# Sixteen small loads, a limit on products between weight tiles, and a norm that uses TensorE

## The chip, the cores and the metric

The kernel runs on one core of one Trainium2 chip. The metric is the device time of one execution in microseconds. TensorE (PE) multiplies, VectorE (DVE), ScalarE (ACT) and GpSimd (POOL) do the element work, and SyncE (SP) issues most of the DMA transfers between device memory and the on-chip memories.

## The reference, cut to what matters

One inference step of a one-layer decoder trunk, in float32. 1032 tokens (1024 new ones of a prompt and 8 single samples) with 2048 features each:

```
mod = silu(c) @ w_ada + b_ada;  shift, scale, gate = split(mod, 3)
h = rmsnorm(x, norm_g) * (1 + scale) + shift
z = h @ w_in                       # 2048 x 8208; the last 16 columns are the logits
...                                # short convolutions, gated delta rule over 8 heads
y = concat(y_a, o) @ w_out;  x = x + gate * y;  return rmsnorm(x, final_norm_g), states
```

`rmsnorm` divides each token by the root of the mean of its squared features. `w_ada` is 2048 x 6144; its first 4096 columns give shift and scale, which h needs, and which depend on no token.

## The kernel before, in words

Features lie on the 128 partitions, in 16 blocks k of 128, and tokens along the free dimension. The tokens are worked in two halves, the first of 512. A product of full precision is three passes on PE: each operand is split in a high part (`whi`, `hh`) and a remainder (`wlo`, `hl`), and high by high, high by remainder and remainder by high are added in PSUM; `passes` is such a triple. ACT makes the high part of a weight tile (`raw` to `whi`), POOL or DVE the remainder (`split_w`). Up to four `raw` tiles are loaded ahead (`Stream.ahead`).

The order of all instructions is written by a planner at build time (`_Order`): it keeps a model of each engine's free time, of the DMA lanes and of each tile's readiness, and side generators (`spawn`) are stepped when their time has come in that model. `_transfer` gives a transfer's modelled time: 290 GB/s for long pieces, 210 for pieces of 512 bytes, 66 for some columns of `w_in`. Each engine executes its own list in order; SP too issues its loads in order, and a load waits for its buffer and for the completion counter that it is to use, of which there are eight for all DMAs.

The ramp is the part around the change. First the 16 blocks of the first half of x are loaded, and `norm` squares them on ACT and adds the squares on DVE into `acc`. `rstd_of` then sums `acc` over the partitions on PE, takes the power -1/2 on POOL, writes the result on the diagonals of `dg` (DVE), and spreads it over all partitions by a product with ones (PE); ACT copies it to `rstd`.

Meanwhile 64 tiles of `w_ada`, `wat`, 512 KB each, stream in with up to nine in flight (`load_ada`). The ramp has ten steps of one or two feature blocks, (0), (1), (2, 3), ... (12, 13), (14), (15). For a step PE multiplies the conditioning by four or eight tiles into `ps`, ACT copies it to `ev`, PE sums four row groups (`selada`), DVE adds the biases (`sh`, `s1`), and `make_h` makes hh and hl of the step's blocks: x times rstd (DVE), scale and shift (ACT and DVE), remainder (DVE). Each h block brings seven triples, of seven output columns that are accumulated in seven PSUM tiles through the whole ramp (`first_products`). `fill` puts such triples into PE's list ahead of a `wat` product, for as long as the planner expects the tile not to have landed.

The logits' 16 columns of `w_in` (`lr`, 2048 rows of 64 bytes) are loaded in the ramp's third step by one DMA that ACT issues; they are used at the ramp's end, as `wlt`.

Of the kernel before, what the change touches and what calls it, by code (L numbers as in the profile page):

```python
# [8 lines left out]
F32 = mybir.dt.float32  # L9
F32R = mybir.dt.float32r  # L10
AF = mybir.ActivationFunctionType
ALU = mybir.AluOpType
# [79 lines left out]
class _Order:  # L92
# [11 lines left out]
    def __init__(self):  # L104
        self.free = dict.fromkeys(("P", "V", "S", "G", "Y", "SH", "YH"), 0.0)
        self.seen, self.slots, self.side, self.busy = {}, {}, [], []
        self.step_end = 0.0
        self.port = {"V": [], "G": []}
        self.lanes, self.lane = [0.0] * 8, 0
        self.pinned = set()  # L110

    @property
    def now(self):
# [198 lines left out]
class _Engine:  # L312
# [15 lines left out]
    def enter(self, op, args, kw, aps, r):  # L328
        od = self.od
        out = [aps[0]] + ([kw["accum_out"]] if kw.get("accum_out") is not None else [])  # L330
        ins = aps[1:] if len(out) == 1 else [a for a in aps[1:] if a is not out[1]]
        n = max(_size(a) for a in aps)
        psum = any("PSUM" in str(a.space) for a in aps)
        one = len([a for a in ins[1:] if _size(a) == 1 and n > 1])
        if op == "dma_start":
            od.move(self.key, ins[0], out[0], _transfer(ins[0], out[0]))
            return
        if self.key == "V":
            if op in ("tensor_scalar", "tensor_copy", "memset"):
# [44 lines left out]
def _trunk(ctx, tc, nc, xT, w_in, w_ada, w_out, pack, consts, vecs, csq, ssm, yT, cap, cqp, ssp, cas, cqs, sss):  # L384
# [76 lines left out]
    def rstd_of(acc, n, out, now=False):  # L461

        nf, w = n // P, n % P
        sm = tp.tile([P, 8], F32, tag="rs", name="rsm")
        if w:
            G.memset(sm[:], 1.0)
        yield [acc[:, :n], 2 * MARGIN]
        while held["ch"]:
            yield 0.2
        ps = ch_tile()  # L470
        for c in range(nf):
            mm(ps[:, c:c + 1], acc[:, c * P:(c + 1) * P], ones[:, 0:1], start=True, stop=True)
        if w:
            mm(ps[:w, nf:nf + 1], acc[:, nf * P:n], ones[:, 0:1], start=True, stop=True)
            V.tensor_scalar(sm[:w, nf:nf + 1], ps[:w, nf:nf + 1], 1.0 / D, EPS, ALU.mult, ALU.add)
        V.tensor_scalar(sm[:, :nf], ps[:, :nf], 1.0 / D, EPS, ALU.mult, ALU.add)
        yield
        nc_ = nf + (1 if w else 0)
        G.tensor_tensor(sm[:, :nc_], sm[:, :nc_], nhalf[:, :nc_], ALU.pow)
        yield  # L480
        dg = tp.tile([P, WH], F32, tag="fx", name="dg", bufs=FX)
        V.tensor_tensor(dg[:, :nf * P].rearrange("p (c i) -> p c i", i=P), ident.unsqueeze(1).to_broadcast([P, nf, P]),
                        sm[:, 0:nf].unsqueeze(2).to_broadcast([P, nf, P]), ALU.mult)
        if w:
            V.tensor_scalar(dg[:w, nf * P:n], ident[:w, :w], sm[:w, nf:nf + 1], None, ALU.mult)
        yield
        p2 = ch_tile()
        mm(p2[:, :nf * P], ones[:], dg[:, :nf * P], start=True, stop=True)
        if w:
            p3 = p2[:, nf * P:n] if n <= 512 else ch_tile()[:, :w]  # L490
            mm(p3, ones[:w, :], dg[:w, nf * P:n], start=True, stop=True)
        S.activation(out[:, :nf * P], p2[:, :nf * P], AF.Copy)
        if w:
            S.activation(out[:, nf * P:n], p3, AF.Copy)
        if now:
            return p2
        yield
# [37 lines left out]
    b1 = cp.tile([P, NK], F32, name="b1")  # L535
    V.tensor_scalar(b1[:], pkv("bada", 16, 16), 1.0, None, ALU.add)

    def make_h(k, xt, n, hh, hl):

        t = tp.tile([P, WH], F32, tag="tm", name="ht")  # L540
        V.tensor_tensor(t[:, :n], xt[:, :n], rstd[:, :n], ALU.mult)
        S.activation(hh[:, :HT], t[:, :HT], AF.Identity, bias=sh[:, k, 0:1], scale=s1[:, k, 0:1])
        V.tensor_scalar(t[:, :HT], t[:, :HT], s1[:, k, 0:1], sh[:, k, 0:1], ALU.mult, ALU.add)
        if n > HT:
            V.tensor_tensor(t[:, HT:n], t[:, HT:n], s1[:, k, 1:9], ALU.mult)
            V.tensor_tensor(t[:, HT:n], t[:, HT:n], sh[:, k, 1:9], ALU.add)
            V.tensor_copy(hh[:, HT:n], t[:, HT:n])
        V.tensor_tensor(hl[:, :n], t[:, :n], hh[:, :n].bitcast(F32), ALU.subtract)
# [13 lines left out]
    class Stream:  # L562
# [26 lines left out]
                self.ahead()  # L589
                yield 0.3  # L590

        def ahead(self, split=True):

            while True:
                if self.loaded < min(self.split + RAW, len(self.todo)):
# [2 lines left out]
                        SY.dma_start(raw[:, a:b, :], src)  # L598
                    self.raws.append(raw)
                    self.loaded += 1  # L600
                elif split and self.split < min(self.freed + SPL, self.loaded) and (
                        self.eager or self.split < self.used + 2 or self.landed()):
                    whi = wp.tile([P, 4, P], F32R, tag="whi", name="whi", bufs=SPL)
                    wlo = wp.tile([P, 4, P], F32R, tag="wlo", name="wlo", bufs=SPL)
# [1 line left out]
                    self.raws[self.split] = None  # L606
                    self.done.append((whi, wlo))
                    self.split += 1
                else:
                    return  # L610

# [769 lines left out]
    def fx_tile(name):  # L1381
        return tp.tile([P, WH], F32, tag="fx", name=name, bufs=FX)

    def norm():
        for k in range(NK):
            if k == 0:
                S.activation(acc[:, :HT], xs0[k][:, :HT], AF.Square)
            else:
                sqt = fx_tile("sqt")
                S.activation(sqt[:, :HT], xs0[k][:, :HT], AF.Square)  # L1390
                V.tensor_tensor(acc[:, :HT], acc[:, :HT], sqt[:, :HT], ALU.add)
        yield from rstd_of(acc, HT, rstd)
        normed.append(True)
    normed = []

    hs = []
    with ExitStack() as pools:
# [35 lines left out]
                        yield  # L1433
        rw, queue, done = {}, [], 0

        def fill(t):

            while od.now < t and queue and od.ready(hs[queue[0][0]][1], False) <= od.now:
                if next(queue[0][1], True):
                    queue.pop(0)  # L1440

        for _ in range(4):
            load_ada()
        ws.ahead(split=False)
        for _ in range(4, ADA):
            load_ada()
        od.spawn(norm())
# [1 line left out]
        for step, (f, nf) in enumerate(steps):  # L1449
            ps = tp_tile()  # L1450
            while done < len(units) and units[done][0] == f:
                _, _, s_, k0, nk = units[done]
                wt = wats[done]
                fill(max(od.ready(wt[:], False), od.ready(ps[:], True) if k0 == 0 and s_ == 0 else 0.0))
                for k in range(k0, k0 + nk):
                    j = k % 4
                    mm(ps[32 * j:32 * j + 32, s_ * nf * P:(s_ + 1) * nf * P], sc[:, k, :],
# [2 lines left out]
                wats[done] = None  # L1460
                done += 1
                load_ada()
                if done < len(units) and units[done][0] == f:
                    pump()
            ev = tp.tile([P, WH], F32, tag="zr", name="ev")
            S.activation(ev[:, :2 * nf * P], ps[:, :2 * nf * P], AF.Copy)
            pump()
# [7 lines left out]
                V.tensor_scalar(s1[:, k, :], ps[:, o:o + 9], b1[:, k:k + 1], pkv("ng", k, 1), ALU.add, ALU.mult)  # L1475
            od.first(ps_g, "tp", ps)
            if step == 0:
                while not normed:
                    od.advance()
                pss = [mm_tile(), mm_tile(), mm_tile(), tp_tile(), ch_tile(), o_tile(), ch_tile()]  # L1480
            if f % 4 == 0:
                hs += h_quad()
            for k in range(f, f + nf):
                make_h(k, xs0[k], HT, *hs[k])
                xs0[k] = None
            queue.append((f + nf - 1, first_products(step)))
            if step == 2:
                S.dma_start(cs[:, EARLY:], consts[:, EARLY:LATE])
                lr_ = fx_tile("lr")
                lr = lr_[:, :256].rearrange("p (k n) -> p k n", n=16)  # L1490
                S.dma_start(lr, w_in[:, 8192:8208].rearrange("(k p) n -> p k n", p=P))
        for _, g in queue:
            for _ in g:
                pass
        S.activation(wl[:, :, 0:16], lr, AF.Copy)
        V.tensor_tensor(wl[:, :, 16:32], lr, wl[:, :, 0:16].bitcast(F32), ALU.subtract)
        ramp = [[p] for p in pss]
        od.spawn(ws.run())

    resd = dp.tile([NK, P, HT], F32, name="resd", bufs=1)  # L1500
# [81 lines left out]
    for half in range(2):  # L1582
# [3 lines left out]
        with ExitStack() as pools:  # L1586
# [100 lines left out]
            if half == 0:  # L1687
# [12 lines left out]
                def next_h():  # L1700

                    for _ in range(2):
# [6 lines left out]
                        make_h(k, x1s[k], WH, *quad[-1][k % 4])  # L1709
# [135 lines left out]
```

## Time and profile before

| | us |
|---|---|
| median of 3 runs | 2210.68 (2208.65 to 2213.19) |
| the profiled execution | 2215.43 |
| its span | 2213.4 |
| PE busy | 2127.4 |
| DVE busy | 1254.3 |
| ACT busy | 829.3 |
| POOL busy | 823.4 |

The span goes from the first to the last instruction on the chip. Busy times of engines lie beside each other and don't sum to the span. In rows of the trace, `a<-b,c` names the tile written and those read; an arrow in brackets names what ended the idle time before an instruction.

### The profile page before, as it was taken

What the parts mean: (1) busy time and instruction counts of PE and PEld (TensorE: products, weight loads), DVE (VectorE), ACT (ScalarE), POOL (GpSimd) and SP (SyncE); (2) the same over time, 40 slices, a digit from 0 to 9 for tenths busy, and PEclk for the clock granted to TensorE, in tenths of its full rate; (3) what the DMA queues carried; (4) which work ended last, traced back from release to release, by engine and by line L of the source; (5) the groups of instructions that cost most, each with busy time, mean ns of one, the idle gap of its engine ahead of it and who ended that gap; (6) DMA issues with size and microseconds to landing.
All of it is one profiled execution on the core that took longest, in us unless ns stands there. A gap on an engine that the chain in (4) does not pass through costs nothing. (4 is left out here: it accounts for less than half of the span.)

```text
span 2213.4 us, 40425 instructions
## 1 busy us (share of the span) xinstructions
PE 2127.4 (96%) x15033; PEld 1865.4 (84%) x15033; DVE 1254.3 (57%) x3664; ACT 829.3 (37%) x1887; POOL 823.4 (37%) x800
## 2 busy tenths in 40 slices
PE   5889999999999999999999999999999999999997
PEld 3457777777777788877889999999999999999996
DVE  3325658637768466258315648657576576335545
ACT  3223434333444333343324334333343333334553
POOL 1122334333333344432434333344333433344444
PEclk9899999999999999999999999999999999999998
DMA  9892685789554455875444565466574445878776
GB/s 291 246 292 58 129 160 144 135 124 144 116 133 89 95 97 94 73 143 187 151 120 101 117 128 113 111 111 107 97 100 82 95 100 96 87 90 230 212 219 202
DMA packets 507318, 299.65 MB, mean 135 GB/s; under 512 B 37361, under 2 KB 486641, under 8 KB 507121
## 3 DMA queue, kind: packets, MB, share of 16 engines
q1 hardware_dynamic: 482352, 285.17, 61.2%
q10 hardware_dynamic: 24768, 11.90, 2.3%
q8 instruction: 118, 1.93, 0.4%
q14 instruction: 80, 0.65, 0.1%
HBM read 277.06 MB, written 19.94 MB: 134 GB/s over the span
## 5 line engine op out<-in xcount | busy, mean ns | idle before, releaser
L322 POOL TENSOR_TENSOR wlo<-raw,whi 128x512 fp32r<-128x512 f32 x528 | 707.0, 1341 | 1279.5 <-ACT whi L322 1105.2
L371 PE MATMUL mm<-hh,whi 128*128 128x264 f32 (+1 forms) x3008 | 975.0, 324 | 9.4 <-DVE y L322 3.8
L371 PE MATMUL mm<-hl,whi 128*128 128x264 f32 (+1 forms) x3008 | 972.7, 323 | 6.5 <-DVE hl L322 6.4
L371 PE MATMUL mm<-hh,wlo 128*128 128x264 f32 (+1 forms) x3008 | 971.0, 323 | 0.5 <-POOL wlo L322 0.5
L322 ACT ACTIVATE whi<-raw 128x512 fp32r<-128x512 f32 x672 | 418.1, 627 | 622.8 <-PE mm L371 349.7
L371 PEld LDWEIGHTS mm<-hh,whi 128*128 128x128 f32 x3008 | 569.1, 189 | 58.8 <-issue 6.9
L371 PEld LDWEIGHTS mm<-hl,whi 128*128 128x128 f32 x3008 | 569.5, 189 | 48.4 <-DVE hl L322 8.9
L371 PEld LDWEIGHTS mm<-hh,wlo 128*128 128x128 f32 x3008 | 569.1, 189 | 41.7 <-POOL wlo L322 1.4
L371 PE MATMUL mm<-yhi,wlo 128*128 128x512 f32 (+2 forms) x768 | 247.9, 323 | 6.3 <-DVE wlo L322 4.7
L371 PE MATMUL mm<-yhi,whi 128*128 128x512 f32 (+2 forms) x768 | 246.1, 320 | 1.3 <-ACT whi L322 1.3
L371 PE MATMUL mm<-ylo,whi 128*128 128x512 f32 (+2 forms) x768 | 246.0, 320 | 0.0
L322 DVE TENSOR_TENSOR ob<-tb,xb 128x62 f32<-128x62 f32 (+30 forms) x992 | 195.6, 237 | 2.6 <-DMA tb<-ub 2.6
L322 DVE TENSOR_TENSOR xb<-xb,ob 128x62 f32<-128x62 f32 (+30 forms) x992 | 196.2, 238 | 0.0
L322 DVE TENSOR_TENSOR wlo<-raw,whi 128x512 fp32r<-128x512 f32 x144 | 110.1, 769 | 133.8 <-ACT whi L322 133.0
L371 PEld LDWEIGHTS mm<-yhi,wlo 128*128 128x128 f32 x768 | 144.4, 188 | 21.7 <-DVE wlo L322 6.7
L371 PEld LDWEIGHTS mm<-yhi,whi 128*128 128x128 f32 x768 | 144.5, 188 | 12.7 <-ACT whi L322 1.6
L371 PEld LDWEIGHTS mm<-ylo,whi 128*128 128x128 f32 x768 | 144.6, 188 | 12.6 <-issue 1.0
L322 DVE SCALAR_TENSOR_TENSOR kq<-zr,pk,kq 128x512 f32<-128x512 f32 x96 | 99.6, 1037 | 3.4
L322 DVE SCALAR_TENSOR_TENSOR res<-mm,ga,xr 128x512 f32<-128x512 f32 (+2 forms) x48 | 27.3, 568 | 109.1 <-PE mm L371 101.8
L371 PE MATMUL tpt<-wat,sc 128*32 128x256 f32 (+1 forms) x640 | 44.9, 404 | 32.9 <-DMA wat<-in_w_ada 29.4
L322 DVE TENSOR_TENSOR acc<-acc,sqt 128x512 f32<-128x512 f32 (+3 forms) x75 | 56.2, 751 | 24.2 <-ACT sqt L322 22.5
L322 DVE SCALAR_TENSOR_TENSOR rt<-cht,gt_neg,v 128x128 f32<-128x128 f32 x56 | 19.6, 350 | 81.0 <-PE cht L371 81.0
(401 smaller groups left out, 1974.7 us busy)
## 6 DMA issues: line engine op xcount, KB each, us to landing
raw<-in_w_in SPq DMA_DIRECT2D x488, 256.0 KB, 5.1
raw<-in_w_out SPq DMA_DIRECT2D x160, 256.0 KB, 3.1
wat<-in_w_ada SPq DMA_DIRECT2D x64, 512.0 KB, 7.7
gw<-in_w_ada SPq DMA_DIRECT2D x64, 256.0 KB, 6.0
tb<-ub ACTq DMA_DIRECT2D x16, 512.0 KB, 6.7
raw<-in_w_in SPq DMA_DIRECT2D x48, 128.0 KB, 6.0
sl<-in_ssm SPq DMA_DIRECT2D x12, 512.0 KB, 6.4
x1s<-in_xT SPq DMA_DIRECT2D x16, 260.0 KB, 5.3
```

The source lines that it names most:

```text
L322: r = f(*args, **kw)
L371: r = self.pe.matmul(out, lhsT, rhs, **kw)
```

## The change

- The planner gets a factor `rings` on every transfer's modelled time, 0.87 during the ramp and 1.0 after it.
- `rstd_of`, which five norms use, no longer makes `dg`: PE transposes each group of 128 values, read with a step of zero as a 128 x 128 tile, and so gets them on all partitions.
- In `norm` the squares of blocks 2, 5, 8 and 11 are summed by PE (a product with the identity) in PSUM, and DVE adds this sum once.
- The multiplication of x by rstd leaves `make_h` for `scaled`; in the ramp it is issued before the `ev` copy, and in the first step it reads the transposes' PSUM tile, not `rstd`. One weight tile is split when the first norm is done.
- `fill` takes a limit: at most three triples ahead of a `wat` product; ahead of a step's first product, while its `ps` tile isn't free, there is none.
- The logits' columns come in sixteen loads of 128 rows (8 KB), issued by SP, one after every third `wat` load from the seventeenth tile used.

```diff
-            od.move(self.key, ins[0], out[0], _transfer(ins[0], out[0]))
+            od.move(self.key, ins[0], out[0], _transfer(ins[0], out[0]) * od.rings)
...
-        dg = tp.tile([P, WH], F32, tag="fx", name="dg", bufs=FX)
-        V.tensor_tensor(dg[:, :nf * P].rearrange("p (c i) -> p c i", i=P), ident.unsqueeze(1).to_broadcast([P, nf, P]),
-                        sm[:, 0:nf].unsqueeze(2).to_broadcast([P, nf, P]), ALU.mult)
-        if w:
-            V.tensor_scalar(dg[:w, nf * P:n], ident[:w, :w], sm[:w, nf:nf + 1], None, ALU.mult)
-        yield
         p2 = ch_tile()
-        mm(p2[:, :nf * P], ones[:], dg[:, :nf * P], start=True, stop=True)
+        for c in range(nf):
+            mm(p2[:, c * P:(c + 1) * P], sm[:, c:c + 1].to_broadcast([P, P]), ident, is_transpose=True)
...
-    def make_h(k, xt, n, hh, hl):
-
+    def scaled(xt, n, r):
         t = tp.tile([P, WH], F32, tag="tm", name="ht")
-        V.tensor_tensor(t[:, :n], xt[:, :n], rstd[:, :n], ALU.mult)
+        V.tensor_tensor(t[:, :n], xt[:, :n], r[:, :n], ALU.mult)
+        return t
+
+    def make_h(k, t, n, hh, hl):
+
...
+            if k in PSQ:
+                mm(ps[:], ident, sqt[:, :HT], start=(k == PSQ[0]), stop=(k == PSQ[-1]))
+                continue
+            V.tensor_tensor(acc[:, :HT], acc[:, :HT], sqt[:, :HT], ALU.add)
+            if k == NK - 3:
+                V.tensor_tensor(acc[:, :HT], acc[:, :HT], ps[:], ALU.add)
+        normed.append((yield from rstd_of(acc, HT, rstd, True)))
+    PSQ, normed = (2, 5, 8, 11), []
...
-        def fill(t):
-
-            while od.now < t and queue and od.ready(hs[queue[0][0]][1], False) <= od.now:
+        def fill(t, most=1000):
+
+            while most and od.now < t and queue and od.ready(hs[queue[0][0]][1], False) <= od.now:
                 if next(queue[0][1], True):
                     queue.pop(0)
+                most -= 1
...
-                fill(max(od.ready(wt[:], False), od.ready(ps[:], True) if k0 == 0 and s_ == 0 else 0.0))
+                if k0 == 0 and s_ == 0:
+                    fill(od.ready(ps[:], True))
+                fill(od.ready(wt[:], False), 3)
...
                 load_ada()
+                k = done - 16
+                if 0 <= k < 48 and k % 3 == 0:
+                    k //= 3
+                    if k == 0:
+                        lr_ = fx_tile("lr")
+                        lr = lr_[:, :256].rearrange("p (k n) -> p k n", n=16)
+                    SY.dma_start(lr[:, k, :], w_in[k * P:(k + 1) * P, 8192:8208])
                 if done < len(units) and units[done][0] == f:
                     pump()
+            if step == 0:
+                while not normed:
+                    od.advance()
+                ws.ahead(1)
+            ts = []
+            for k in range(f, f + nf):
+                ts.append(scaled(xs0[k], HT, rstd if step else normed[0]))
+                xs0[k] = None
             ev = tp.tile([P, WH], F32, tag="zr", name="ev")
             S.activation(ev[:, :2 * nf * P], ps[:, :2 * nf * P], AF.Copy)
...
             if step == 2:
                 S.dma_start(cs[:, EARLY:], consts[:, EARLY:LATE])
-                lr_ = fx_tile("lr")
-                lr = lr_[:, :256].rearrange("p (k n) -> p k n", n=16)
-                S.dma_start(lr, w_in[:, 8192:8208].rearrange("(k p) n -> p k n", p=P))
```

## Rows read from the trace of the kernel before

**Rows 1.** The page, part 1: busy time, share of the span, instructions.
```profile
PE 2127.4 (96%) x15033; PEld 1865.4 (84%) x15033; DVE 1254.3 (57%) x3664; ACT 829.3 (37%) x1887; POOL 823.4 (37%) x800
```

**Rows 2.** Windows: stretch and length; busy of each engine, PE clock, DMA share, GB/s.
```profile
200.00:400.00 200.00, 199.32 (x1226) 156.94 (x1226) 136.21 (x412) 78.93 (x188) 73.45 (x74) 1.00 0.62 135
...
600.00:800.00 200.00, 193.64 (x993) 156.10 (x992) 141.12 (x454) 83.31 (x211) 74.96 (x75) 0.99 0.48 103
...
0.00:63.96 63.96, 34.85 (x295) 21.50 (x295) 21.38 (x42) 19.11 (x32) 7.48 (x14) 0.87 1.02 299
63.96:194.94 130.98, 114.69 (x760) 73.18 (x757) 37.82 (x70) 30.45 (x48) 28.01 (x25) 0.93 0.76 215
```

**Rows 3.** Timeline of PE at the ramp's end: start, duration, engine, line, operation, tiles.
```profile
194.94 0.40 PE L371 MATMUL mm<-hh,wlt 128*128 128x512 f32 x1
```

**Rows 4.** Windows of 2 us.
```profile
62.00:64.00 2.00, 2.00 (x21) 0.71 (x13) 1.11 (x3) 0.89 (x2) 0.00 (x0) 0.50 1.10 349
...
84.00:86.00 2.00, 2.00 (x13) 1.01 (x12) 0.00 (x0) 0.00 (x0) 0.00 (x0) 0.76 0.09 25
```

**Rows 5.** Waits of SP's queue, 40 to 90: total us, times, longest.
```profile
SPq L322 <- DMA lr<-in_w_in: 14.1, 1, 14.1
```

**Rows 6.** The tile lr: its load (issue ns, first and last start), and its landing.
```profile
L322 ACTq DMA_DIRECT2D lr<-in_w_in x1: 618/618/618, 63.2 to 63.2; - x1
...
DMA to landing us min/median/max: 21.6/21.6/21.6
```

**Rows 7.** Timeline of SP's queue: two issues of w_ada tiles.
```profile
84.90 0.37 SPq L322 DMA_DIRECT2D wat<-in_w_ada  x1
...
156.93 0.37 SPq L322 DMA_DIRECT2D wat<-in_w_ada  x1
```

**Rows 8.** Waits of PE, 63.9 to 194.9: total us, times, longest.
```profile
PE mm L371 <- DVE hl L322: 5.7, 5, 1.9
PE tpt L371 <- DMA wat<-in_w_ada: 4.0, 2, 3.5
PE tpt L371 <- ACT ev L322: 2.3, 1, 2.3
PE mm L371 <- ACT hh L322: 1.9, 2, 1.2
PE tpt L371 <- PE tpt L371: 1.9, 2, 1.0
```

**Rows 9.** Timeline of ACT: the copy ahead of the late ev.
```profile
100.62 0.63 ACT L322 ACTIVATE whi<-raw 128x512 fp32r<-128x512 f32 x1 [1.79 <-DMA raw<-in_w_in]
```

**Rows 10.** Windows of 10 us; the granted clock is third from the end.
```profile
80.00:90.00 10.00, 8.25 (x50) 4.59 (x50) 0.00 (x0) 0.11 (x1) 0.00 (x0) 0.83 0.66 189
...
100.00:110.00 10.00, 7.25 (x52) 4.25 (x52) 4.58 (x10) 3.26 (x5) 2.13 (x2) 0.66 1.09 330
...
150.00:160.00 10.00, 10.00 (x52) 5.89 (x51) 0.00 (x0) 1.47 (x3) 2.58 (x2) 0.84 0.98 271
```

**Rows 11.** DMA queues in 68 to 72: packets, MB, share of 16 engines.
```profile
q1 hardware_dynamic: 188, 0.19, 14.7%
q10 hardware_dynamic: 580, 0.04, 8.2%
```

**Rows 12.** Timeline of DVE: the first norm's adds; one multiplication by rstd.
```profile
7.43 11.84 DVE L322 TENSOR_TENSOR acc<-acc,sqt 128x512 f32<-128x512 f32 x15 [1.09 <-ACT sqt L322]
...
141.58 0.68 DVE L322 TENSOR_TENSOR ht<-x,rstd 128x512 f32<-128x512 f32 x1
```

**Rows 13.** Timeline of the last norm: dg, and its product with ones.
```profile
2201.81 0.42 DVE L322 TENSOR_TENSOR dg<-cs,rsm 128x256 f32<-128x256 f32 x1 [0.81 <-POOL rsm L322]
...
2202.29 1.22 PE L371 MATMUL cht<-dg,ones 128*128 128x256 f32 x2 [1.49 <-DVE dg L322]
```

**Rows 14.** Groups by line, shapes apart: busy us, mean ns of one.
```profile
L371 PE MATMUL tpt<-cs,kq 128*128 128x128 f32 x128 | 19.2, 272 | 0.0
...
L371 PE MATMUL cht<-dg,ones 128*128 128x512 f32 x6 | 4.1, 774 | 0.0
```

More of the change, by code (lines that the diff above doesn't have):

```diff
@@ L110, in __init__ @@
         self.pinned = set()
+        self.rings = 0.87
     @property
@@ L480, in rstd_of @@
         yield
-        dg = tp.tile([P, WH], F32, tag="fx", name="dg", bufs=FX)
-        V.tensor_tensor(dg[:, :nf * P].rearrange("p (c i) -> p c i", i=P), ident.unsqueeze(1).to_broadcast([P, nf, P]),
-                        sm[:, 0:nf].unsqueeze(2).to_broadcast([P, nf, P]), ALU.mult)
-        if w:
-            V.tensor_scalar(dg[:w, nf * P:n], ident[:w, :w], sm[:w, nf:nf + 1], None, ALU.mult)
-        yield
         p2 = ch_tile()
-        mm(p2[:, :nf * P], ones[:], dg[:, :nf * P], start=True, stop=True)
+        for c in range(nf):
+            mm(p2[:, c * P:(c + 1) * P], sm[:, c:c + 1].to_broadcast([P, P]), ident, is_transpose=True)
         if w:
             p3 = p2[:, nf * P:n] if n <= 512 else ch_tile()[:, :w]
-            mm(p3, ones[:w, :], dg[:w, nf * P:n], start=True, stop=True)
+            mm(p3, sm[:w, nf:nf + 1].to_broadcast([w, P]), ident[:w, :w], is_transpose=True)
         S.activation(out[:, :nf * P], p2[:, :nf * P], AF.Copy)
@@ L590, in run, with ahead @@
                 yield 0.3
-        def ahead(self, split=True):
+        def ahead(self, most=SPL):
             while True:
@@ L600, in ahead @@
                     self.loaded += 1
-                elif split and self.split < min(self.freed + SPL, self.loaded) and (
+                elif most and self.split < min(self.freed + SPL, self.loaded) and (
                         self.eager or self.split < self.used + 2 or self.landed()):
@@ L1384, in norm @@
     def norm():
+        ps = ch_tile()
         for k in range(NK):
@@ L1387, in norm @@
                 S.activation(acc[:, :HT], xs0[k][:, :HT], AF.Square)
[L1388 to L1394, printed above, removed]
+                continue
+            sqt = fx_tile("sqt")
+            S.activation(sqt[:, :HT], xs0[k][:, :HT], AF.Square)
+            if k in PSQ:
+                mm(ps[:], ident, sqt[:, :HT], start=(k == PSQ[0]), stop=(k == PSQ[-1]))
+                continue
+            V.tensor_tensor(acc[:, :HT], acc[:, :HT], sqt[:, :HT], ALU.add)
[3 more added lines that the diff above has]
+    PSQ, normed = (2, 5, 8, 11), []
     hs = []
@@ L1434, in _trunk @@
         rw, queue, done = {}, [], 0
-        def fill(t):
-            while od.now < t and queue and od.ready(hs[queue[0][0]][1], False) <= od.now:
+        def fill(t, most=1000):
+            while most and od.now < t and queue and od.ready(hs[queue[0][0]][1], False) <= od.now:
                 if next(queue[0][1], True):
                     queue.pop(0)
+                most -= 1
         for _ in range(4):
             load_ada()
-        ws.ahead(split=False)
+        ws.ahead(0)
         for _ in range(4, ADA):
@@ L1477, in _trunk @@
             if step == 0:
-                while not normed:
-                    od.advance()
                 pss = [mm_tile(), mm_tile(), mm_tile(), tp_tile(), ch_tile(), o_tile(), ch_tile()]
@@ L1482, in _trunk @@
                 hs += h_quad()
-            for k in range(f, f + nf):
-                make_h(k, xs0[k], HT, *hs[k])
-                xs0[k] = None
+            for k, t in zip(range(f, f + nf), ts):
+                make_h(k, t, HT, *hs[k])
             queue.append((f + nf - 1, first_products(step)))
@@ L1497, in _trunk @@
         ramp = [[p] for p in pss]
+        od.rings = 1.0
         od.spawn(ws.run())
@@ L1708, in next_h @@
                             yield 0.2
-                        make_h(k, x1s[k], WH, *quad[-1][k % 4])
+                        make_h(k, scaled(x1s[k], WH, rstd), WH, *quad[-1][k % 4])
                         hs.append(quad[-1][k % 4])
```

## The prediction

> **What bounds the kernel now.** I read the page's busy shares first: TensorE (PE) is busy 96% of the span, so little can be won unless one stretch holds the idle 4% [rows 1]. Then the windows: PE idles 0.7 us in 200 to 400, 6.4 in 600 to 800, but far more at the start [rows 2]. Before 63.96 us it is busy 34.85 of 63.96 us while the DMA share is 1.02: that start is bound by w_ada's transfers, and PE starves. From 63.96 to 194.94 us (the first product with the logits' columns, `mm<-hh,wlt`, by which all first products are done [rows 3]) PE is busy 114.69 of 130.98 us, so it idles 16.3, at a mean clock of 0.93, and the DMA share is only 0.76. The reader is to see that in this second stretch neither engine nor DMA is full: something keeps work from PE. All that the change can win lies there and at the very end of the program.
>
> The cause is in the 2-us windows: 349 GB/s at 62 to 64, 25 at 84 to 86 [rows 4]. At 70 us SP, which issues every weight load in order, stops: its longest wait is 14.1 us for the one load of the logits' columns [rows 5], issued by ScalarE at 63.2 us and landing 21.6 us later [rows 6]; its next load goes out at 84.90 [rows 7]. It waits because completion counters are handed round over the DMAs, and the one that its next load needs belongs to that slow load. The last w_ada tile is issued only at 156.93 us [rows 7].
>
> What it costs PE: in 63.96 to 194.94 PE waits 4.0 us for w_ada tiles (3.5 of them in one piece, at the end of the hole) and 2.3 for an `ev` copy [rows 8]. The `ev` wait belongs to the hole as well: ScalarE copies `ev` right behind a `whi` that waited 1.79 us for its own raw tile, late because SP was stopped [rows 9]. The other waits, hl 5.7, hh 1.9 and PE on PE 1.9, are those of a step's boundary. Each stretch of idling is followed by the lower clock: the granted clock is 0.83 in 80 to 90, 0.66 in 100 to 110, 0.84 in 150 to 160 [rows 10], that is, parts of these run at 1.2 GHz and not 2.4, and lose 1.7, 3.4 and 1.6 us.
>
> **The change, part by part** (against the profiled execution: 2215.43 us, span 2213.4; the median of the runs is 2210.68, 4.75 lower).
>
> 1. *The single load goes.* The hole's waits go (4.0 + 2.3 = 6.3), and the low clock after two of them (1.7 + 3.4 = 5.1): minus 11.4 us. Bounds: minus 4.0, the direct waits alone, and minus 16, if all PE idling of the stretch is the hole's. DMA transfers are late next, but far from the end: the last w_ada issue is 38 us before 194.94, and in the meantime PE works off a backlog.
>
> 2. *Sixteen loads of 8 KB come into SP's queue*, one for every three w_ada tiles. They total 2048 pieces of 64 bytes, as before. No row shows them in this queue. Below: 580 of these packets take 8.2% of 16 engines in 4 us [rows 11], 9 ns each, so 128 of them on 16 engines are 0.07 us a load and 1.1 us in all. Above: the old load's whole 21.6 us [rows 6] over sixteen is 1.35 us each, 21.6 in all, if w_ada stands still behind each one; the same rows show that it nearly did: w_ada's queue moved 188 packets in 4 us beside 580 of the small ones. Between them I take 0.7 us a load on the DMA, the middle, 11 us. But PE pays only where it has run dry of landed tiles, and nine tile buffers stand between; with a third of the loads felt I take plus 4 us. The issue itself (0.37 us as a tile's [rows 7], 5.9 in all) I cost at nothing, since SP is ahead of the landings; behind it in SP's queue stand the next `raw` and w_ada loads, and for these PE waits.
> The rows say that 64-byte pieces, not the number of loads, set the price. The Trainium skill, "DMA: Bandwidth & Descriptors", section Rules for kernel authors, says to coalesce many small transfers into one large one, since under 64 KB one pays mostly overhead; that speaks against cutting 128 KB into sixteen. By it sixteen small loads would each carry a completion of their own, and the median would come out at 2213.8, by the upper end above; the trace agrees only that small pieces are dear, the one large transfer being here the one that stops SP.
>
> 3. *At most three triples between tiles, and the planner's transfers times 0.87.* This reorders PE's stream and adds or removes nothing. Per two-k step 14 triples face 8 tiles, so three a tile never starves the step; before, only the planned landing limited them. A full-rate tile (524 KB at 349 GB/s, [rows 4]) lands in 1.5 us, and the planner had priced it at 290 GB/s; 0.87 brings it to 333, near the row. Bounds: minus 5, plus 5; I take 0.
>
> 4. *x times rstd is made ahead of the ev copy.* It takes the 0.68 us multiply [rows 12] out of the chain from `sh`/`s` to hh and hl, once for the first k of a step and again in front of the second. Seven waits on hl and hh sum to 7.6 us [rows 8]; I take half of it, 3.5, and half of the low clock behind the boundary at 142 to 149 (1.6), 0.8: minus 4.3. Bounds: 0 if the boundary then waits for `ev`, minus 10.
>
> 5. *First norm.* VectorE loses four of 15 adds and gains one from PSUM; its adds, 15 in 11.84 us with their gaps, stand from 7.43 to 19.27 [rows 12], so at most 3 x 0.79 = 2.4 us go, and with them `dg`, the ones-product and the copy of rstd behind them. Four squares on PE lie ahead of its first w_ada product, where it has nothing else. I cost all of it at 0: w_ada's transfers, at a share of 1.02 until 63.96, are the cover. Without this cover it would be worth 4 us (2.4, and the 1.70 of step 6).
>
> 6. *The other norms.* Each transpose replaces a share of `dg` and the ones-product. The last norm stands on the path to the end: from `dg`'s start at 2201.81 to the ones-product's end at 2203.51 it is 1.70 us [rows 13]. Transposes of 128x128 are 272 ns alone and 19.2/128 = 0.15 in a row [rows 14]: two take 0.42, so minus 1.3. Two norms of 512 tokens amid a full PE: 4.1/3 = 1.37 us [rows 14] against 0.6, minus 1.5 together. Bounds of all three: minus 1.5, minus 4.
>
> Sum: -11.4 + 4 + 0 - 4.3 + 0 - 1.3 - 1.5 = -14.5, so 2200.9 for a profiled execution and 2196.2 for the median. After 195 us the rest moves as a block, because PE has no slack there.
>
> **Rivals.**
> *A. The small loads hold the ring (slower).* Every one of the sixteen stops the w_ada behind it for 1.35 us, and the planner, which prices it at about a tenth of that, puts w_ada's products in PE's stream where the tile isn't there, with ready triples behind. For it: 188 packets in 4 us [rows 11]. Against: nine buffers, and the 38 us of backlog. Then +21.6 replaces +4: 2213.8, and two more drops of the clock like that of 100 to 110 add 6.8, about 2221. It decides from 1.2 us a load that reaches PE.
> A rule by which it would come about: the Trainium skill, "DMA: Bandwidth & Descriptors", section Queues, rings and completion order, says that one engine's descriptors are consumed in ring order within a queue, while different queues take turns. The old load had a queue of its own; the new ones stand in w_ada's. Whether taking turns was cheaper no run here shows.
> *B. Only the direct wait goes.* PE is then limited at the boundaries, the `ev` and low clock at 100 come back there, and the multiply moved ahead gains nothing: 4.0 + 1.7 + 1.3 = 7, so 2203.7. For it: the hl waits, five, aren't all in the hole's wake. Against: the `whi` that waited for a raw tile [rows 9].
> *C. The gain is lost later.* The new order after the ramp costs what the ramp won: PE's idle time of 200 us differs by 5.7 us between two stretches [rows 2]; two such differences give back 11.4: 2207.6.
> *D. All idling and low clock of the stretch go* (16.3, and 0.07 x 130.98 = 9.2; with the last norm 26.8): 2183.9.
>
> **How the numbers follow.** Forecast 0.60, A 0.09, B 0.18, C 0.08, D 0.05. 0.2% is 4.4 us, about what can be told from no change: faster means below 2206.3. Faster: 0.60, D's 0.05 and most of B, 0.15, make 0.80; within: C and the rest of B, 0.11; slower: A, 0.09. The range goes from D, 2184, to C, 2208; the forecast's own range is 2187 to 2203.
>
> **What would show it.** Right: no SP wait over 3 us for the logits' load; DMA above 250 GB/s in every 10 us from 46 to 140; the first `mm<-hh,wlt` at 176 to 184 us and not 194.94; hl waits at half of 5.7; between the last rsm and rf about 0.5 us and not 1.75. Step 2 is wrong if PE's waits for w_ada after 64 us exceed 6 us, step 4 if hl and hh waits stay at 7.6. The prediction fails if the first `wlt` product comes after 190 us, or if it comes early and PE's idle time after 200 us grows by as much.

## The result, and the profile after

The changed kernel takes 2178.61 us (median of 4 runs, 2177.39 to 2183.28) against 2209.66 for the kernel before on the same chip (4 runs); the ratio is 0.9868, with a 95% interval of 0.9853 to 0.9882. So the direction was right, but the gain is twice the forecast one: 0.0132 x 2209.66 = 29 us instead of 14.5, and the time lies below the range.

Its profiled execution took 2179.28 us. The page's busy shares of the changed kernel:

```profile
PE 2116.6 (97%) x15045; PEld 1858.7 (85%) x15045; DVE 1243.7 (57%) x3653; ACT 829.3 (38%) x1887; POOL 826.4 (38%) x801
```

PE is busy 10.8 us less than in [rows 1] though it has twelve instructions more: 7.9 us less in the second stretch below, where it had been granted a low clock, 2.6 more in the first, and 5.4 less behind the ramp. The windows show it (changed kernel; length, then busy time and count of PE, PEld, DVE, ACT, POOL, then PE clock, DMA share, GB/s). The split is at 59.82 us, the start of a product `mm<-hh,whi` as 63.96 is in [rows 2], and at 169.30, the ramp's end; the two stretches behind it, the 2-us and the 10-us windows are those of [rows 2, 4, 10].

```profile
0.00:59.82 59.82, 37.43 (x296) 21.01 (x296) 21.67 (x40) 20.42 (x34) 7.90 (x15) 0.83 1.03 303
59.82:169.30 109.48, 106.75 (x769) 68.75 (x766) 38.35 (x67) 28.17 (x45) 28.64 (x26) 1.00 0.92 266
200.00:400.00 200.00, 199.71 (x1275) 156.74 (x1274) 141.19 (x471) 78.01 (x194) 73.39 (x75) 1.00 0.66 138
600.00:800.00 200.00, 196.22 (x1044) 158.66 (x1042) 123.46 (x389) 76.00 (x181) 72.98 (x74) 0.99 0.49 98
62.00:64.00 2.00, 2.00 (x21) 0.80 (x19) 1.27 (x3) 0.00 (x0) 0.00 (x0) 1.00 1.10 352
84.00:86.00 2.00, 2.00 (x15) 1.29 (x15) 0.00 (x0) 0.60 (x1) 1.28 (x1) 1.00 1.11 338
80.00:90.00 10.00, 10.00 (x69) 6.56 (x68) 2.21 (x7) 3.27 (x5) 2.46 (x3) 1.00 1.11 345
100.00:110.00 10.00, 10.00 (x68) 6.08 (x67) 5.04 (x10) 3.16 (x5) 2.55 (x2) 1.00 1.11 338
150.00:160.00 10.00, 10.00 (x104) 8.20 (x103) 4.71 (x9) 2.24 (x4) 1.29 (x1) 1.00 0.37 92
```

The reader is to see three things. The second stretch is 21.5 us shorter (109.48 against 130.98): PE idles 2.7 us in it, not 16.3, and at a full clock it is busy 106.75 us, not 114.69. The hole in the transfers is gone: 338 GB/s at 84 to 86, not 25. And the gain is kept: PE idles 0.3 and 3.8 us in the two stretches after the ramp, less than before.

The ramp ends with the first product by the logits' columns. PE's timeline of the changed kernel has it here:

```profile
169.28 0.40 PE L372 MATMUL mm<-hh,wlt 128*128 128x512 f32 x1
```

That is 25.7 us before [rows 3], where the forecast had 11.7 for the ramp (11.4 - 4 + 4.3). What PE still waits for between 59.8 and 169.3 us (line and tile waited for; us in total, times, longest):

```profile
PE mm L372 <- DVE hl L323: 1.8, 3, 1.0
PE tpt L372 <- PE tpt L372: 1.0, 1, 1.0
```

There is no wait for a w_ada tile, for `ev` or for hh any more [rows 8]. SP's waits from 46 to 160 us (first and fourth line of that list) name the logits' tile nowhere; it stands mostly for a free buffer:

```profile
SPq L323 <- PE tpt L372: 16.2, 19, 3.4
...
SPq L323 <- DMA wat<-in_w_ada: 4.0, 7, 0.9
```

The logits' tile itself (min, median, max of the issues in ns, first and last start; then the landing), where [rows 6] had one landing of 21.6 us:

```profile
L323 SPq DMA_DIRECT2D lr<-in_w_in x16: 495/1168/1863, 59.3 to 156.0; - x16
...
DMA to landing us min/median/max: 3.7/6.2/8.0
```

In SP's timeline the last two w_ada tiles go out at 140.64 us, not at 156.93 [rows 7]:

```profile
140.64 2.57 SPq L323 DMA_DIRECT2D wat<-in_w_ada  x2
```

And the last norm has its two transposes where [rows 13] had `dg` and the product with ones (chain of waits):

```profile
2166.28 0.70 POOL rsm L323
...
2167.03 0.45 PE cht L372 x2
```

One thing must be known about the rows of before: a second profile of that kernel has a span of 2206.0 us, not 2213.4, with the ramp's end at 194.4 us, as in [rows 3]. So some 7 us of the difference between the profiles of [rows 2] and of the changed kernel lie after the ramp and belong to the one execution. I compare ramps by their end (194.4 to 169.3, minus 25.1) and totals by the ratio of runs.

### The profile page after: what moved, and what is told of

It reads as the page before. It is cut to its first block, busy times and chain, and to the rows that moved or that the text cites. A ratio compares the mean times of both kernels' runs of the same rounds, so it can differ in the third digit from the quotient of the medians.

```text
span 2177.5 us, 40451 instructions
## 1 busy us (share of the span) xinstructions
PE 2116.6 (97%) x15045; PEld 1858.7 (85%) x15045; DVE 1243.7 (57%) x3653; ACT 829.3 (38%) x1887; POOL 826.4 (38%) x801
## 5 line engine op out<-in xcount | busy, mean ns | idle before, releaser
L323 DVE TENSOR_TENSOR acc<-acc,sqt 128x512 f32<-128x512 f32 (+3 forms) x71 | 54.7, 773 | 26.1 <-ACT sqt L323 25.1
L323 ACT ACTIVATE u<-cht,sm 128x128 f32<-128x128 f32 x64 | 23.5, 367 | 89.1 <-DVE u L323 76.0
```

Source lines behind the costliest of these rows:

```text
L323: r = f(*args, **kw)
```

## The experiments

All ratios are to the kernel before on the same chip. "Ramp end" is the start of the first `mm<-hh,wlt` in the profiled execution (for the kernel before, in its second profile), one profile each.

| kernel | median us | ratio, 95% interval | ramp end |
|---|---|---|---|
| before | 2209.66 | 1 | 194.4 |
| changed | 2178.61 | 0.9868, 0.9853 to 0.9882 | 169.3 |
| before + sixteen loads | 2198.17 | 0.9949, 0.9930 to 0.9968 | 182.8 |
| before + new order | 2200.3 | 0.9963, 0.9948 to 0.9978 | 183.0 |
| before + both | 2186.3 | 0.9898, 0.9875 to 0.9920 | 168.3 |
| before + transposes | 2203.25 | 0.9971, 0.9959 to 0.9983 | 190.2 |
| before, one load of wide rows | 2201.04 | 0.9974, 0.9960 to 0.9988 | 184.7 |
| before, sixteen loads in a burst | 2210.27 | 1.0005, 0.9994 to 1.0017 | 191.4 |
| changed, one load | 2193.32 | 0.9932, 0.9910 to 0.9955 | 179.4 |
| changed, loads doubled | 2184.89 | 0.9887, 0.9871 to 0.9903 | 171.9 |
| changed, loads on ACT's queue | 2187.16 | 0.9903, 0.9888 to 0.9917 | 177.2 |
| changed, loads late | 2180.04 | 0.9872, 0.9849 to 0.9896 | 171.2 |
| changed, no limit | 2180.66 | 0.9872, 0.9856 to 0.9888 | 169.4 |
| changed, factor 1 | 2183.07 | 0.9882, 0.9867 to 0.9897 | 171.1 |
| changed, neither | 2184.45 | 0.9888, 0.9875 to 0.9901 | 175.8 |
| changed, late multiplication | 2179.24 | 0.9865, 0.9848 to 0.9881 | 170.6 |
| changed, neither, late multiplication | 2197.11 | 0.9949, 0.9934 to 0.9964 | 185.1 |
| changed, `dg` back | 2183.6 | 0.9886, 0.9871 to 0.9900 | 169.4 |
| changed, adds on DVE | 2180.41 | 0.9874, 0.9858 to 0.9890 | 169.3 |

**A second look at the kernel before**, unchanged.

> The kernel before once more, for a second profile. If the profiled execution that the prediction rests on was a usual one: first wlt product at 194 to 196. If it was slow by its 4 to 6 us over the median in the ramp: 188 to 191; if after the ramp: 194 to 196, and the rest shorter by 5.

The ramp is a usual one, and what the first profile took longer lay behind it, as told above. Its windows from 60 us to the ramp's end are the base for what follows:

```profile
60.00:194.40 134.40, 116.48 (x776) 72.99 (x773) 38.72 (x72) 31.30 (x49) 27.87 (x25) 0.94 0.76 218
```

PE idles 17.9 us, and loses about 9.6 more to the clock, as 106.9 us suffice for the same work at a full clock (below).

**The sixteen loads alone**, put into the kernel before.

```diff
+                k = done - 16
+                if 0 <= k < 48 and k % 3 == 0:
+                    ...
+                    SY.dma_start(lr[:, k, :], w_in[k * P:(k + 1) * P, 8192:8208])
...
-                S.dma_start(lr, w_in[:, 8192:8208].rearrange("(k p) n -> p k n", p=P))
```

> The kernel before with only the logits' load cut in sixteen on SP's queue; limit, factor and norms as before. Theory L (the one load's stop is the loss): 2190 or below, 20 us or more of the 31, first wlt product at 178 or earlier. Theory O (the order of products and tiles is the larger part): 2198 to 2206, 4 to 11 us gained, the low clock at 100 and the hl waits of 5.7 us stay, first wlt product at 184 to 190.

Measured: 11 us less in the runs, 11.6 in the ramp. That is the size that theory O gave, but the low clock at 100, which it kept, is gone (1.00 in 100 to 110), and the ramp ends before its 184. From 60 us on, the window and PE's waits:

```profile
60.00:182.80 122.80, 111.29 (x776) 71.53 (x769) 42.40 (x73) 30.73 (x49) 26.90 (x24) 0.97 0.82 237
```

```profile
PE mm L371 <- DVE hl L322: 6.8, 5, 1.9
PE mm L371 <- ACT hh L322: 2.7, 3, 1.2
```

Of the 17.9 us of idling 6.4 are gone, and 5.2 of PE's busy time with its low clock. That is near step 1's forecast (6.3 and 5.1), in part by luck: the waits for w_ada tiles go (6.1 us in the second profile of before, none here), of the `ev` waits only half (2.1 to 1.0), and those on hl and hh grow from 6.8 to 9.5. What the loads cost is not seen here, only the sum of steps 1 and 2. What is left (11.5 idle) is a boundary's: hl 6.8, hh 2.7, and 1.0 each for `ev` and for PE's own results. PE's timeline of this kernel at the boundary of (10, 11):

```profile
127.09 0.95 PE L371 MATMUL tpt<-cs,ev 128*128 128x10 f32 x8
...
129.47 1.93 PE L371 MATMUL tpt<-wat,sc 128*32 128x256 f32 x32
...
133.17 0.49 PE L371 MATMUL mm<-hh,whi 128*128 128x512 f32 x1 [0.72 <-ACT hh L322]
135.57 0.50 PE L371 MATMUL mm<-hl,whi 128*128 128x512 f32 x1 [1.91 <-DVE hl L322]
...
138.61 0.63 PE L371 MATMUL mm<-hh,whi 128*128 128x512 f32 x1
```

At 127.09 PE sums the row groups, from which the next hh and hl are made; those of the step's second block are there 6 and 8.5 us later. In between PE does the last six products in stock, four w_ada tiles on end (x32) and one triple of the first block; then it has nothing, waits 0.72 and 1.91, and the products behind it take 0.63 us and not 0.40: the granted clock is 0.59 in 136 to 138, most of it at 1.2 GHz and not 2.4.

**The order (limit and factor), on top of it and alone.**

```diff
+            od.move(self.key, ins[0], out[0], _transfer(ins[0], out[0]) * od.rings)
...
+                if k0 == 0 and s_ == 0:
+                    fill(od.ready(ps[:], True))
+                fill(od.ready(wt[:], False), 3)
```

> The kernel before with the sixteen loads, the limit of three triples and the factor 0.87; norms and the multiplication by rstd as before. Theories L and O: within 6 us of the changed kernel, 2179 to 2185. Theory N (first norm and the multiplication ahead of ev give 10 us or more): 2188 or slower, with hl and hh waits of 7 us as before.

> The kernel before with the limit of three triples and the factor 0.87 alone; one load of the logits' columns, norms as before. Theory O as a part of its own: 9 to 12 us faster than before, 2195 to 2198, as it gave on top of the sixteen loads. If the order pays only where the stop is gone: within 5 us of before.

Measured: on top of the loads another 11 us in the runs and 14.5 in the ramp; alone 8 and 11.4. The kernel with both lies 1.3 us above the range of theories L and O and below that of N, and its waits on hl and hh are gone (0.2 us), against N; the order alone lies between its two cases. The window from 60 us, and PE's timeline at the same boundary, of the kernel with both:

```profile
60.00:168.30 108.30, 106.91 (x765) 68.24 (x766) 40.06 (x69) 30.51 (x49) 29.32 (x26) 1.00 0.93 268
```

```profile
118.31 0.95 PE L372 MATMUL tpt<-cs,ev 128*128 128x10 f32 x8
119.11 0.48 PE L372 MATMUL tpt<-hh,whi 128*128 128x512 f32 x1
...
120.69 1.07 PE L372 MATMUL tpt<-wat,sc 128*32 128x256 f32 x16
121.69 0.50 PE L372 MATMUL cht<-hh,whi 128*128 128x512 f32 x1
...
122.58 0.64 PE L372 MATMUL tpt<-wat,sc 128*32 128x256 f32 x8
123.15 0.50 PE L372 MATMUL cht<-hh,whi 128*128 128x512 f32 x1
```

Behind the same step's `cs,ev` product tiles alternate with triples, and no row has a wait in brackets. The same triples in another order: fewer were spent ahead of the tiles before, and some are left for the boundary. All idling but 1.4 us goes, and all the low clock: 10.1 + 4.4 = 14.5. Why the runs give only 11 of it is not shown. This kernel has the old norms and the late multiplication, and its ramp ends 1.0 us before that of the changed one: on top of loads and order, the other parts of the change gain nothing in the ramp.

**Taking the halves of the order out of the changed kernel, and the multiplication.**

```diff
-                fill(od.ready(wt[:], False), 3)
+                fill(od.ready(wt[:], False))
```
```diff
-        self.rings = 0.87
+        self.rings = 1.0
```
```diff
-            for k, t in zip(range(f, f + nf), ts):
-                make_h(k, t, HT, *hs[k])
+            for k in range(f, f + nf):
+                make_h(k, scaled(xs0[k], HT, rstd), HT, *hs[k])
```

> The changed kernel without the limit of three triples; the factor 0.87 stays. Theory O1 (the limit keeps triples back for the step boundaries): 2184 to 2192, hl, hh and ev waits of 7 us or more between 60 and the first wlt product. Theory O2 (the factor does it, since the planner then fills less anyway): within 3 us of the changed kernel.

> The changed kernel with transfers modelled at their old times; the limit stays. O1: within 3 us of the changed kernel. O2: 2184 to 2192, with PE running out of triples at the boundaries.

> The changed kernel with the multiplication by rstd back behind the row sums, and from rstd, not PSUM. If it was worth the 4.3 us of the prediction: 2182 to 2185 and hl and hh waits up by 3 us or more. If the boundaries are covered by triples that were kept back: within 2 us.

> The changed kernel without the limit and with transfers modelled at their old times, so both halves of the new order undone at once. Theory R (either half alone does the same work, so that undoing one shows nothing): 2187 to 2192, first wlt product at 178 or later, hl waits back above 5 us. Theory M (the multiplication made ahead of ev covers the boundaries, and the order is worth little here): 2180 to 2184.

> As the run with the old order, and the multiplication by rstd back behind the row sums too. Theory R: within 2 us of the run with the old order alone. Theory M: 5 us or more slower than it, near the kernel before with sixteen loads less the transposes' 4 us, 2190 to 2196.

Each edit alone moves the ramp's end by 0.1 to 1.8 us and the runs by some 3 us at most. Together they are dear. The halves of the order stand in for each other: with the multiplication ahead the ramp ends at 169.4 with the factor alone, at 171.1 with the limit alone, at 175.8 with neither. So it isn't shown that the limit of three is what keeps triples back; either half does most of it. The kernel with neither (2184.45) lies between theories R and M; with the late multiplication too it is 13 us slower, as M had it. Ramp ends by the order and the place of the multiplication, all with sixteen loads:

| | multiplied ahead | multiplied late |
|---|---|---|
| new order | 169.3 | 170.6 |
| old order | 175.8 | 185.1 |

In the order of the table's lower row, PE's waits from 60 us to 195: first the old order with the multiplication ahead, then without it.

```profile
PE mm L372 <- DVE hl L323: 3.7, 3, 1.3
PE tpt L372 <- PE tpt L372: 2.9, 3, 1.0
```

```profile
PE mm L372 <- DVE hl L323: 6.8, 5, 1.9
PE mm L372 <- ACT hh L323: 2.7, 3, 1.2
```

So there is one loss, of some 16 us, the boundary's. The multiplication ahead shortens the chain that PE waits for and saves 9.3 of it; the order gives PE other work in that time and saves 14.5. With the order in place the multiplication still saves 1.3; with the multiplication in place the order still saves 6.5. By taking only one edit out one would have called each nearly worthless.

**The one load put back into the changed kernel.**

```diff
-                    SY.dma_start(lr[:, k, :], w_in[k * P:(k + 1) * P, 8192:8208])
...
+                S.dma_start(lr, w_in[:, 8192:8208].rearrange("(k p) n -> p k n", p=P))
```

> The changed kernel with the logits' columns in one load on ScalarE's queue again. Theory L: the stop of 14 us comes back, 2198 or slower, first wlt product at 185 or later. Theory O: 2184 to 2192, the stop is there but nine tiles and the evenly spread triples cover most of it, first wlt product at 174 to 182.

Measured: 10.1 us later in the ramp and about 14 in the runs, between the two theories, with the ramp's end where O had it. SP stands again for that load:

```profile
SPq L323 <- DMA lr<-in_w_in: 13.7, 1, 13.7
```

**What makes the one load dear: wide rows, doubled, another queue, late, a burst.**

```diff
-                S.dma_start(lr, w_in[:, 8192:8208].rearrange("(k p) n -> p k n", p=P))
+                S.dma_start(lr_[:, :256], xT[0:P, 0:256])
```

> The kernel before, its one load on ScalarE's queue taken from 128 rows of 1 KB of x in place of 2048 pieces of 64 bytes: the logits' weights are then other numbers, the transfer is 128 KB still. Theory L, with the pieces of 64 bytes as the reason: no SP wait over 3 us there, time within 4 us of the kernel before with sixteen loads. If the stop is of the load as such (its place, its queue), the wait of 14 us stays and the time stays at 2206 to 2214.

With 128 rows of 1 KB (of x, so this kernel leaves out the logits' weights) in place of 2048 of 64 bytes the load lands after 6.3 us, SP waits 0.4 us for it, and the ramp ends 9.7 us earlier: the stop comes of the 64-byte pieces, not of the load's place or queue. The runs gain only 5.7 (3 to 9); why less than the sixteen loads, stays open.

```diff
+                    SY.dma_start(lr2[:, k, :], w_in[k * P:(k + 1) * P, 8192:8208])
```

> The changed kernel with each of the sixteen small loads issued twice, the second into a tile that nothing reads. Prediction's step 2 (0.25 us of PE time a load): plus 4 us, 2181 to 2185. Rival A (1.2 us and more a load): plus 19 us or more, 2198. If the buffers hide them wholly: within 2 us.

Sixteen more loads, whose data nobody reads, cost 2.6 us in the ramp, 0.16 each (4 in the runs, 0.26 each, which are known to some 3 us). The forecast had 0.25 each.

```diff
-                    SY.dma_start(lr[:, k, :], w_in[k * P:(k + 1) * P, 8192:8208])
+                    S.dma_start(lr[:, k, :], w_in[k * P:(k + 1) * P, 8192:8208])
```

> The changed kernel with the sixteen loads on ScalarE's queue, so on another ring than w_ada's. If a ring of their own spares w_ada's tiles: 2 to 4 us faster, 2174 to 2177. If ScalarE's copies and ev are held by the waits for completion counters, slower by 5 us or more, with ScalarE's queue waiting. Otherwise within 2 us.

On ACT's queue the same loads cost 8 us more than on SP's. PE's waits (59 to 177 us) and SP's (50 to 165):

```profile
PE tpt L372 <- DMA wat<-in_w_ada: 8.7, 11, 1.3
```

```profile
SPq L323 <- DMA wat<-in_w_ada: 16.1, 16, 2.1
SPq L323 <- DMA lr<-in_w_in: 7.1, 6, 2.1
```

SP stands again for loads that another engine issued, six times, and w_ada tiles come late; the expectation had looked for the wait on ACT's side. So a queue of its own spares w_ada nothing here.

```diff
-                k = done - 16
-                if 0 <= k < 48 and k % 3 == 0:
-                    k //= 3
+                k = done - 49
+                if 0 <= k < 16:
```

> The changed kernel with the sixteen small loads one behind each of the last sixteen w_ada products, where most of w_ada has been issued, and not spread over the last 48. If sixteen of them cost PE 2 to 4 us by what they hold of w_ada, as their doubling suggests: 1 to 3 us faster, 2176 to 2178, first wlt product at 166.5 to 168.5. If their price is SP's own issue time or nothing: within 1 us.

One behind each of the last sixteen w_ada products: no better (0.9872 against 0.9868, the ramp 1.9 us longer); the 1 to 3 us that were expected didn't come.

```diff
-                S.dma_start(lr, w_in[:, 8192:8208].rearrange("(k p) n -> p k n", p=P))
+                for k in range(NK):
+                    SY.dma_start(lr[:, k, :], w_in[k * P:(k + 1) * P, 8192:8208])
```

> The kernel before, with its one load of logits' columns replaced, at the same place in the second step, by sixteen loads of 128 rows each, issued one right behind another on SP's queue: cut as in the change, not spread. Theory S (the 2048 pieces cost the DMA engines the same however they are cut, and only their spreading lets the buffers of w_ada hide them): a hole of 8 us or more in the transfers around 80 us, with the windows of 2 us below 150 GB/s, TensorE waits for w_ada tiles or gets a low clock behind it, first wlt product at 189 to 195, 2204 to 2210 us. Rival C (cutting does it: loads of 128 rows go through cheaply even together): no window of 10 us from 60 to 130 below 250 GB/s, no SP wait over 3 us, first wlt product at 181 to 186, 2196 to 2202 us.

In the kernel before, the sixteen loads right behind each other gain nothing (1.0005), as theory S had it: what helps is that they are spread, not that they are cut. SP's timeline, windows, and the queue from 66 to 78 us (packets, MB, share of 16 engines), of this kernel:

```profile
60.30 12.84 SPq L322 DMA_DIRECT2D lr<-in_w_in  x16
73.83 7.36 SPq L322 DMA_DIRECT2D wat<-in_w_ada  x5
```

```profile
68.00:70.00 2.00, 2.00 (x15) 1.08 (x14) 0.00 (x0) 0.25 (x1) 0.73 (x1) 1.00 0.08 8
...
76.00:78.00 2.00, 2.00 (x10) 1.64 (x9) 1.08 (x3) 0.82 (x1) 0.00 (x0) 1.00 0.06 6
78.00:80.00 2.00, 0.43 (x2) 0.00 (x0) 0.38 (x1) 0.00 (x0) 0.00 (x0) 1.00 0.26 64
80.00:82.00 2.00, 0.00 (x0) 0.00 (x0) 0.00 (x0) 0.00 (x0) 0.00 (x0) 0.72 1.06 372
```

```profile
q1 hardware_dynamic: 1486, 0.13, 7.5%
```

SP waits for the counters of these loads 2.1 us in all. But with such waits issuing the loads takes 0.80 us each (0.43 in the median without them), 12.8 us in which no w_ada load goes out, and the bytes of those issued from 73.83 on flow only from about 79. From 66 to 78 the DMA engines are 7.5% busy with 1486 packets. So the price of 64-byte pieces is time in a queue and not DMA capacity: on end about 0.8 us a load, spread between tiles 0.16 in the ramp. The transfers go on beside the spread ones (350 GB/s from 60 to 70 us in the changed kernel, with loads issued at 59.3 and 64.5); that the nine tiles in flight are the reason is argued, not tested.
The gap from 73.83 to 79 agrees with the Trainium skill, "DMA: Bandwidth & Descriptors", section Queues, rings and completion order, by which an engine consumes a queue's descriptors in ring order: w_ada's stood behind the small ones.

In the kernel before, the one load had another queue than w_ada's. Yet the transfers fell before SP stopped (14.1 us up to 84.90, so at 70.8). A 2-us window of that kernel, and the w_ada tile that it issued between 68 and 72 us (at 68.72; size, us to landing):

```profile
68.00:70.00 2.00, 2.00 (x15) 1.14 (x14) 0.00 (x0) 0.49 (x1) 1.29 (x1) 1.00 0.23 60
```

```profile
wat<-in_w_ada SPq DMA_DIRECT2D x1, 512.0 KB, 16.7
```

The median of its w_ada tiles is 7.7. So tiles already in flight were slowed beside the small pieces too, and the hole is not SP's stop alone. How much each of the two costs, no run separates.

**The norms.**

```diff
-        for c in range(nf):
-            mm(p2[:, c * P:(c + 1) * P], sm[:, c:c + 1].to_broadcast([P, P]), ident, is_transpose=True)
+        dg = tp.tile([P, WH], F32, tag="fx", name="dg", bufs=FX)
+        V.tensor_tensor(...)
+        mm(p2[:, :nf * P], ones[:], dg[:, :nf * P], start=True, stop=True)
```

> The changed kernel with dg and the product with ones in all five norms, in place of the transposes. By the prediction's step 6: 2181 to 2182.5, of which 1.2 us in the last norm. If the transposes carry the 6 to 8 us that separate the kernel with loads and order from the changed one: 2185 to 2188.

> The kernel before with the transposes in place of dg in all five norms and nothing else. Prediction's step 6: 2.8 us, with at most 1 more from the first norm. If the run with dg put back told its whole worth: 4 us, give or take 2.

`dg` back in all five norms costs 4.0 us in the runs, between its two cases, and nothing in the ramp (169.4). The transposes alone, in the kernel before, gain 6.4 (3.8 to 9.1), more than the 2.8 of step 6, with a ramp 4.2 us shorter in its one profile. There PE waits 2.9 us for w_ada tiles, not 6.1; why, I can't say.

```diff
-    PSQ, normed = (2, 5, 8, 11), []
+    PSQ, normed = (), []
```

> The changed kernel with all fifteen adds of the first norm on VectorE, none on PE. By the prediction's step 5 (covered by w_ada's transfers): within 2 us. If the first norm is on the path: plus 2 to 4 us, and the first wlt product later by as much.

All the adds on DVE again: the ramp ends at 169.3 us as with PE's help, and the runs can't be told apart. The first product of an h block starts at 32.3 us here, at 32.4 in the changed kernel and at 32.3 in the kernel before.

## Why the prediction was wrong in size

**The step that failed is the third**, "This reorders PE's stream and adds or removes nothing", priced at 0 with bounds of 5 either way. It is worth 11 us in the runs and 14.5 in the ramp on top of the sixteen loads. The sentence is true, but a worth of 0 doesn't follow from it: what was reordered is what PE has to do while a step's hh and hl are made. The waits on them fall from 9.5 us to 0.2 by it, and the low clock behind them goes. The working had shown that something was left over: of 16.3 us idle and 9.2 lost to the clock, step 1 claimed 6.3 and 5.1, step 4 3.5 and 0.8, and nobody the rest, 6.5 and 3.3. A fair bound for an edit that reorders work around a wait would have been all of that wait with the low clock behind it: seven waits on hl and hh, 7.6 us, and two on PE, 1.9 [rows 8], plus the 4.1 of the clock that step 1 didn't claim: 13.6, where 14.5 was measured, the waits on hl and hh having grown to 9.5 with the loads spread.

Point by point:

- Steps 1 and 2, forecast at -7.4, measured -11.6 in the ramp and -11 in the runs. The hole, the waits for w_ada in it and the clock behind them were right; SP's stop is only a part of its cause, as the tile of 16.7 us shows, and half of the `ev` wait stays. Whether step 1 was too small or step 2's 4 us too dear is not shown: doubling the loads gives 2.6 in the ramp and 4 in the runs. Rival A, by which they hold the ring, fell: the burst has its mechanism, at 0.8 us a load, but spread out they cost a fifth of that. The threshold that the forecast gave, 6 us of waits for w_ada, was not touched: there are none.
- The weighing of large against small transfers in step 2 came out as follows: in the changed kernel sixteen loads of 8 KB beat the one of 128 KB by 14 us, and in a burst they equal it. What decided was not the size of a transfer (one of 128 KB in rows of 1 KB stops nothing) but its short rows, with what stood behind them or moved beside them.
- Step 4, forecast at -4.3: 1.3 in the ramp beside the new order and none in the runs, 9.3 in the ramp without it. Its mechanism is there, but step 3 had taken the same loss.
- "Each stretch of idling is followed by the lower clock" is too wide for the rows of before: PE idles 1.6 us in 120 to 130, and the granted clock is 1.00 there and in 130 to 140.
- Step 5, forecast at 0, was right: w_ada's transfers cover the first norm. No edit to it shortens the ramp, nor do all of them together.
- Step 6, forecast at -2.8, measured -4.0 with `dg` put back and -6.4 for the transposes alone, whose interval leaves the forecast out. The last norm is as forecast, 0.45 for the two transposes, where 0.42 was worked out; what the others gain above 1.5 us is within the interval of the first run, and in the second stays open.
- Of the named tests, SP's wait for the logits, the DMA rate (lowest 264 GB/s, at 70 to 80), the hl waits (1.8, under half of 5.7) and the last norm (0.52 us between rsm and rf) came out right, the first `wlt` product not: 169.28, ahead of the 176 to 184 given.
- Rival C, that the gain is lost later, fell, as the windows after 200 us show. What came is nearest to rival D, to which I gave 0.05 because no step that I had priced could bring it.

In sum, by ratios of runs: sixteen loads 11, the order 11, and 7 for the rest, of which the transposes are 4; this makes the 29. The last 7 is the difference of two ratios that are known to 3 and 5 us. Of the 14.5 us that the forecast lacked, 11 are step 3 and 4 are steps 1 and 2. Steps 4 to 6 come to their forecast of 7.1 by luck: step 4 brought none of its 4.3 in the runs. No kernel of the study beats the changed one; the one with the late multiplication equals it.

## What to carry to other kernels

When idle time is left that no step of the sum claims, an edit that reorders work may win it, so its worth is not to be put at zero: look at what the waiting engine did just before the wait, and whether work was spent there that would have filled it. Two edits against one loss, a shorter chain and filler work for it, are in part substitutes; take both out before calling either worthless. A load of many short pieces is to be priced by what is queued behind it and what moves beside it; here it paid to spread it between large ones.

## What the runs showed of the hardware

A few products ahead of the main work were followed by a low clock. Windows from 20 to 30 us, first of the changed kernel, where PE also sums four blocks of squares from 8.47 us on with gaps, then of the one with all adds on DVE:

```profile
20.00:30.00 10.00, 6.82 (x64) 5.24 (x64) 1.38 (x5) 2.34 (x5) 2.27 (x2) 0.50 1.10 248
```

```profile
20.00:30.00 10.00, 6.27 (x63) 4.85 (x62) 3.05 (x6) 3.62 (x7) 3.52 (x4) 1.00 1.10 246
```

With the squares PE is granted 1.2 GHz from 18.5 to 35.6 us, without them 2.4 until 56.7. Before it fell, PE had summed the squares until 15.66 us and then stood 2.8 us for a w_ada tile, as PE's timeline of the changed kernel has it:

```profile
18.47 1.08 PE L372 MATMUL tpt<-wat,sc 128*32 128x128 f32 x16 [2.81 <-DMA wat<-in_w_ada]
```

In 20 to 30 us the granted clock is 0.50 to 0.67 in all eleven profiles with the squares on PE and 0.96 to 1.00 in all nine without them, of which seven have 0.66 to 0.70 in the ten us behind. Whether the gaps in the early work matter is not shown. Both ramps end at 169.3 us: the transfers' share is 1.10 in both, and they set the pace there.
